# Router and shared expert in plain f32 on unsplit rows, logits by token tiles, modulations of the next block on TensorE, short expert lists first

## The chip, the cores and the metric

One core of a Trainium2 chip. The metric is the device time of one execution in microseconds: 3116.91 us is the median of three runs of the kernel before (3116.86 to 3132.91). TensorE is called PE here (PEld its weight loads), VectorE DVE, ScalarE ACT, GpSimd POOL, SyncE SP.

## The reference

Two blocks run one after the other on 512 tokens of 1024 channels, all in f32. The first has a mixer and a mixture of experts, the second two layers of other mixers and an MLP, each with modulations (shift, scale, gate) that are computed from a conditioning vector. What the change touches is the end of the first block:

```
x = x + gt1 * (heads_x @ w_out)                       # mixer's output projection
h = modulate(rmsnorm(x, g_ffn), sh2, sc2)
scores = sigmoid(h @ router_w)                        # 64 experts
... choose 4 of 8 groups of experts, then 6 experts a token, weights sum to 2.5
routed[t] += w[t, e] * swiglu(h[t], w_gate[e], w_up[e], w_down[e])    # 256 hidden
x = x + gt2 * (routed + swiglu(h, s_gate, s_up, s_down))              # shared expert, 256 hidden
```

and the start of the second: `silu(c_2) @ mod_w_2[layer] + mod_b_2[layer]`, 6 x 1024 columns a layer, in which c_2 is one vector of 1024.

## The kernel before, in words

Activations lie with channels on the partitions (8 tiles of 128 channels x 512 tokens). The kernel is written for a framework that orders the instructions of each engine at build time, by program order as the priority; `issue_after(i)` keeps a block's instructions of an engine behind instruction i.

*Split arithmetic.* Most projections take an f32 value as a sum of two reduced parts: `split` (L307 to 310) writes the high part by ACT (L309) and the rest by POOL or DVE (L310), and `mm3` (L336 to 343) makes three matmuls of it (L338, L342, L343). One step is 128 x 128 weights against 512 columns.

*The end of the mixer* (L665 to 690). The output projection runs in two groups g of four output tiles, each in two column halves i (two of the four token tiles each). After a half of the second group, `second_norm` (L1519) and `norm_half` (L1467) make the norm, write h in split form (`mhh`, `mhl`), transpose it to token rows and store these in DRAM (`hrows`). `shared_ahead` loads the router's and the shared expert's weights and splits them.

*The start of the experts* (`moe`, L1303 to 1400). The logits are 24 split steps with the router's 64 columns as weights, a copy `lt` and four transposes (L1340). `route` (L1072 to 1198) picks the experts, sorts the 64 experts by their number of tokens and gives each token its position in each of its experts' lists. After the first lists are built, the shared expert runs in split form (L1382 to 1399): two column halves of gate and up, then the down projection into x, 144 steps in all.

*Lists.* `slots` (L1210 to 1232) builds the lists of up to eight experts at once: a one-hot per expert on DVE (L1216), four small matmuls on PE (L1218), then small DVE instructions to a tile of sources (L1227, read by the gather), a tile of targets (L1229, read by the scatter) and weights. Empty slots have an out-of-range source, and a spare row behind the 512 as target. These tiles have five buffers each. List lengths are fixed by rank, `CAPS`, four experts each, 128 down to 16 slots (3968 slots in all, for 3072 real rows; the two experts of `TWICE` have a second list). 22 lists are long (over 64 slots), 44 short.

*The loop over 66 lists* (L1420 to 1438), in the order of one long and two short. Per list: POOL gathers the rows by indirect DMA (L1249, three lists ahead), PE transposes them (L1265), ACT copies, PE does gate and up (long L1279; short L1274, in two column groups), ACT does Silu (L1281), DVE the gated product `eh` (L1282), PE transposes it (L1287), DVE copies it to `ehT` (L1288), PE does the down projection (L1295 or L1298), ACT and DVE copy it to `ey` (L1299), and POOL adds it to `yrows` in DRAM by an indirect DMA (L1300). Expert weights are 3 tiles of 1 MB each, on SP's queue, through rings of tiles: 7 are to be had before the shared expert ends (`RINGB`, `ringA`), 15 afterwards (with `RINGD`). The groups of lists are given a due iteration, six lists before their first use (L1352 to 1356), with nothing that holds them there.

*Modulations of the second block.* The first 2048 columns of its first layer are eight pieces of 256 (`MODS_B`): their weights pass through the same rings in the loop, and from iteration 48 on DVE makes the dot products (L396) against a row form of the vector that PE spreads over the partitions (`on_rows`, L404). `mod_rows` (L408) and `mod_cols` (L414) are the form on PE that the first block's own modulations use at the start of the kernel: four matmuls of 32 columns of weights against 512, twice, then four small ones that bring the row back to columns.

The functions that the diff touches, with the lines of the profile:

Of the kernel before, what the change touches and what calls it, by code (L numbers as in the profile page):

```python
# [9 lines left out]
F32 = mybir.dt.float32  # L10
# [10 lines left out]
P = 128  # L21
# [21 lines left out]
HLB = 4  # L43
RINGB = 1
RINGD = 8

CAPS = (128, 128, 96, 80, 72, 64, 56, 48, 48, 40, 40, 32, 32, 24, 24, 16)
MODS_B = 8
# [114 lines left out]
def layout(v):  # L163
# [21 lines left out]
    o["mod_w_2"] = two(lambda l: _rows(g["mod_w_2"][l], (256,) * 24))  # L185
# [26 lines left out]
class Kern:  # L212
# [201 lines left out]
    def mod_cols(self, p, pool, out):  # L414

        r = pool.tile([P, T], F32, tag="mdr", name="mdr", bufs=2)
# [76 lines left out]
    def block1_mix(self):  # L493
# [12 lines left out]

        esr = ExitStack()
# [10 lines left out]

        self.sc32 = ax.tile([P, KD, 32], F32, name="sc32")
        nc.gpsimd.memset(self.sc32, 0.0)  # L520
        nc.vector.tensor_copy(self.sc32[:, :, 0:2], sc2)
        self.pick = ax.tile([P, 2], F32, name="pick")
        nc.vector.tensor_reduce(self.pick, self.ident.rearrange("p (q i) -> p i q", i=32)[:, 0:2], axis=AX.X, op=OP.add)
# [146 lines left out]
        self.hl, self.nhl = [hlB] * HLB + [self.hlS] * 2 + [hlB] * 2, 0  # L670
        self.subs = (nc.gpsimd, nc.vector)
        ks = (4, 5, 6, 7, 0, 1, 2, 3)
        for g in range(2):
            ws = [w for j in range(2) for w in self.split_w(self.load_w(I["w_out"], (2 * g + j) * 256, 256))]
            ps = [self.ps(tag=n) for n in ("c00", "c01", "c10", "c11")]
            for i in range(2):
# [7 lines left out]
                if g:  # L684
                    self.second_norm(i)
                    self.norm_half(i)
        self.shared_ahead()
# [384 lines left out]
    def route(self, logits, R):  # L1072
# [120 lines left out]
        nc.gpsimd.tensor_copy(aux[:, :, :, 0], self.C("pidx").unsqueeze(2).to_broadcast([P, NT, NE]))  # L1193
        for t in range(NT):
            nc.gpsimd.memset(aux[:, t, :, 1], float(t))
        nc.gpsimd.memset(aux[:, :, :, 2], 1.0)
# [13 lines left out]
    def slots(self, pos, aux, n, cap, pool, tag, bufs):  # L1210
# [9 lines left out]
        v, a, iv, u = t_("v", n, 6, k=2), t_("a", n, k=2), t_("iv", n, k=2), t_("u", n, k=2)  # L1220
        src, dst, wt = t_("src", n, dt=I32), t_("dst", n, dt=I32), t_("wt", n)
# [10 lines left out]
        return src, dst, wt  # L1232
# [20 lines left out]
    def expert(self, W, dst, wt, xg, pool):  # L1253
# [28 lines left out]
        nc.vector.scalar_tensor_tensor(h, h, wt, up, op0=OP.mult, op1=OP.mult)  # L1282
# [13 lines left out]
        for n, o in enumerate(os_):  # L1296
            for k in () if pair else range(2):
                mm(o, hT[:, k], wd[:, k, n * T:(n + 1) * T], start=k == 0, stop=k == 1)  # L1298
            (nc.vector.tensor_copy if n else nc.scalar.copy)(y[:, n * T:(n + 1) * T], o)  # L1299
        nc.gpsimd.indirect_dma_start(out=self.yrows, out_offset=bass.IndirectOffsetOnAxis(ap=dst, axis=0), in_=y,  # L1300
                                     in_offset=None, bounds_check=T + P - 1, oob_is_err=True, compute_op=OP.add)

    def moe(self):  # L1303
# [6 lines left out]
        nc.gpsimd.tensor_copy(self.trib, self.C("before"))  # L1310
        nc.gpsimd.tensor_copy(self.onesb, self.C("ones"))
        self.spare = cp.tile([P, 1], F32, name="spare")
        nc.gpsimd.tensor_scalar(self.spare, self.C("pidx"), float(T), None, op0=OP.add)
# [3 lines left out]
        self.alias = {"tp": ["c00", "c01"], "gu": ["c10", "c11"], "y": ["ax", "st0", "st1"], "sl": ["dn"]}  # L1317
        ahead = self.pool("ringA", bufs=6, es=es)
        sp = self.sp = self.pool("slots", es=es)
        es1 = self.es1  # L1320
        self.subs = (nc.gpsimd,)
        self.esh.close()
        h = self.h2
        b = self.pool("moe1", es=es1, side="right")
        self.hlM = self.pool("hlM", bufs=1, es=es1, side="right")
# [3 lines left out]
        for x in self.xgs:  # L1329
            nc.gpsimd.memset(x, 0.0)  # L1330
        for i in range(0, T + P, CAP):
            n = min(CAP, T + P - i)
            nc.scalar.dma_start(self.yrows[i:i + n], self.xgs[0][:n])
        Ws = [self.expert_load(I["experts"][e], ahead, nc.scalar) for e in range(FIRST)]
        self.stream = "y"
        lt = b.tile([NE, T], F32, tag="sg_", name="lt", bufs=2)
        nc.scalar.copy(lt, self.mtile(self.rw, 0, h, m=NE))
        lg = self.ps((P, NT, NE))
        for t in range(NT):
            nc.tensor.transpose(lg[:, t], lt[:, t * P:(t + 1) * P], self.ident[:NE, :NE])  # L1340
        self.stream = "sl"
        self.route(lg, R)
        got = {}

        long, short = [e for e in range(FIRST, NE) if CAPS[e // 4] > 64], [e for e in range(NE) if CAPS[e // 4] <= 64]
# [12 lines left out]
        def sl(e, n, b=0):  # L1358
# [5 lines left out]
            for j, x in enumerate(zip(*[[a[:, j:j + 1] for j in range(n)] for a in self.slots(  # L1364
                    lambda j: pos[:, :, j], lambda j, t: R["aux"][:, t, e + j], n, CAPS[e // 4], sp, "s2" if b else "s", 1 if b else 5)])):
                got[e + j, b] = [q[:CAPS[(e + j) // 4]] for q in x]

        sl(0, 4)
# [10 lines left out]
        ring = [self.pool("ringB", bufs=RINGB, es=esb)] * RINGB + [ahead] * 6  # L1379

        self.hl, self.nhl = [self.hlM, self.hlS, self.hlS, self.hlM], 0
        for j in range(2):  # L1382
            self.wgu[j, 1] = self.split_w(self.raws[j][:, :, P:])[0]
# [37 lines left out]
        for i in range(n + 1):  # L1421
            for g in due.pop(i, ()):
                sl(*g)
# [975 lines left out]
```

## Time and profile before

| | |
|---|---|
| time, three runs | 3116.91 (3116.86 to 3132.91) us |
| the profiled execution's own time | 3115.47 us |
| its span in the profile | 3113.7 us |
| mean granted clock of PE | 0.925 |
| PE busy | 2773.6 us (89%), 17250 instructions |
| PEld busy | 2050.8 us (66%) |
| DVE busy | 1574.9 us (51%), 3396 instructions |
| ACT busy | 951.2 us (31%), 1900 instructions |
| POOL busy | 1094.6 us (35%), 839 instructions |

The span in 40 slices of 77.8 us, busy share in tenths (the DMA line is the mean over the 16 DMA engines); the experts are slices 9 to 17, counted from one:

```profile
PE   6999998799888898678998889989989988889998
...
DVE  5877765642111112375856575663748575642224
...
PEclk9999898899999999969999789999899798999999
DMA  5134002469999999831124114453121041212221
```

A stretch's busy shares are averages; what ends last in it is read from the waits and the timeline. Idle time of an engine that others don't wait for costs nothing.

### The profile page before, as it was taken

What the parts mean: (1) busy time and instruction counts of PE and PEld (TensorE: products, weight loads), DVE (VectorE), ACT (ScalarE), POOL (GpSimd) and SP (SyncE); (2) the same over time, 40 slices, a digit from 0 to 9 for tenths busy, and PEclk for the clock granted to TensorE, in tenths of its full rate; (3) what the DMA queues carried; (4) which work ended last, traced back from release to release, by engine and by line L of the source; (5) the groups of instructions that cost most, each with busy time, mean ns of one, the idle gap of its engine ahead of it and who ended that gap; (6) DMA issues with size and microseconds to landing.
All of it is one profiled execution on the core that took longest, in us unless ns stands there. A gap on an engine that the chain in (4) does not pass through costs nothing.

```text
span 3113.7 us, 44073 instructions
## 1 busy us (share of the span) xinstructions
PE 2773.6 (89%) x17250; PEld 2050.8 (66%) x17250; DVE 1574.9 (51%) x3396; ACT 951.2 (31%) x1900; POOL 1094.6 (35%) x839
## 2 busy tenths in 40 slices
PE   6999998799888898678998889989989988889998
PEld 4767887566544444265665677878856656778887
DVE  5877765642111112375856575663748575642224
ACT  4243333311111111133423343322334234433222
POOL 3333333422222222234333235644252243354443
PEclk9999898899999999969999789999899798999999
DMA  5134002469999999831124114453121041212221
GB/s 215 63 113 156 2 2 99 172 185 379 359 356 340 342 349 374 319 124 42 55 82 149 61 55 173 165 178 113 52 82 41 28 149 54 80 70 95 95 95 55
DMA packets 81537, 460.76 MB, mean 148 GB/s; under 512 B 11424, under 2 KB 18240, under 8 KB 35120
## 3 DMA queue, kind: packets, MB, share of 16 engines
q1 hardware_dynamic: 63360, 404.98, 34.6%
q0 software_dynamic: 11312, 31.46, 4.3%
q10 hardware_dynamic: 6656, 21.50, 1.8%
q8 instruction: 136, 2.23, 0.3%
q14 instruction: 73, 0.60, 0.1%
HBM read 434.29 MB, written 27.26 MB: 148 GB/s over the span
## 4 chain that ended last, share of the span: by engine, by line
PE 35%; DVE 9%; DMA 3%; POOL 2%; issue 2%; ACT 2%; ACTq 0%; DVEq 0%; POOLq 0%
PE ps_pj L338 5%; PE ps_pj L342 5%; PE ps_pj L343 5%; PE ps_a L342 4%; PE ps_a L338 4%; PE ps_a L343 4%; DVE rawm L396 2%; DMA rawm<-in_mod_w_dram 2%; PE ps_a L1695 1%; PE ps_m L1947 1%; PE ps_a L2030 1%; PE ps_a L1685 1%; PE ps_a L1718 1%; DVE bs L2328 1%; DVE ba L2332 1%
## 5 line engine op out<-in xcount | busy, mean ns | idle before, releaser
L310 POOL TENSOR_TENSOR wl<-raw,wh 128x1024 fp32r<-128x1024 f32 (+2 forms) x165 | 408.4, 2477 | 663.5 <-ACT wh L309 628.2
L309 ACT CAST wh<-raw 128x1024 fp32r<-128x1024 f32 (+2 forms) x241 | 246.7, 1034 | 562.4 <-PE ps_a L342 397.2
L338 PE MATMUL ps_pj<-lhh,wh 128*128 128x512 f32 (+5 forms) x816 | 326.4, 400 | 1.8 <-ACT wh L309 1.2
L343 PE MATMUL ps_pj<-lhh,wl 128*128 128x512 f32 (+5 forms) x816 | 315.8, 387 | 6.1 <-POOL wl L310 3.6
L342 PE MATMUL ps_pj<-lhl,wh 128*128 128x512 f32 (+5 forms) x816 | 315.5, 387 | 0.0
L396 DVE SCALAR_TENSOR_TENSOR rawm<-rawm,cb 128x1024 f32<-128x1024 f32 x128 | 206.6, 1631 | 92.7 <-DMA rawm<-in_mod_w_dram 75.3
L310 DVE TENSOR_TENSOR wl<-raw,wh 128x1024 fp32r<-128x1024 f32 x76 | 99.2, 1306 | 206.6 <-ACT wh L309 206.5
L1300 POOL DMA_INDIRECT yrows<-ey,sdst x64 | 97.3, 1520 | 279.9 <-DMA yrows<-ey,sdst 143.8
L338 PE MATMUL ps_a<-lhh,wh 128*128 128x512 f32 (+3 forms) x464 | 169.7, 370 | 21.7 <-ACT lhh L470 13.9
L338 PEld LDWEIGHTS ps_pj<-lhh,wh 128*128 128x128 f32 (+2 forms) x816 | 160.1, 196 | 40.3 <-issue 11.6
L343 PEld LDWEIGHTS ps_pj<-lhh,wl 128*128 128x128 f32 (+2 forms) x816 | 159.3, 195 | 39.4 <-POOL wl L310 4.4
L342 PEld LDWEIGHTS ps_pj<-lhl,wh 128*128 128x128 f32 (+2 forms) x816 | 159.9, 196 | 35.4 <-issue 9.0
L1282 DVE SCALAR_TENSOR_TENSOR eh<-eh,swt,ps_c 128x256 f32<-128x256 f32 (+10 forms) x64 | 30.2, 472 | 288.9 <-ACT eh L1281 287.6
L342 PE MATMUL ps_a<-lhl,wh 128*128 128x512 f32 (+3 forms) x464 | 168.8, 365 | 0.9 <-POOL lhl L474 0.6
L1274 PE MATMUL ps_c<-raw,xT 128*48 128x256 f32 (+6 forms) x1408 | 167.5, 387 | 0.0
L343 PE MATMUL ps_a<-lhh,wl 128*128 128x512 f32 (+3 forms) x464 | 167.5, 362 | 0.0
L1279 PE MATMUL ps_c<-raw,xT 128*128 128x256 f32 (+3 forms) x704 | 161.0, 386 | 0.0
L1279 PEld LDWEIGHTS ps_c<-raw,xT 128*128 128x128 f32 (+3 forms) x704 | 118.9, 172 | 47.2 <-issue 9.9
L1249 POOL DMA_INDIRECT xg<-hrows,ssrc x64 | 66.3, 1036 | 233.5 <-PE ps_c L1265 190.5
L1281 ACT ACTIVATE eh<-ps_c 128x256 f32<-128x256 f32 (+10 forms) x66 | 25.1, 380 | 387.2 <-PE ps_c L1279 217.2
L1274 PEld LDWEIGHTS ps_c<-raw,xT 128*48 128x48 f32 (+6 forms) x1408 | 84.9, 117 | 65.3 <-issue 7.3
L2155 POOL TENSOR_TENSOR ffr<-ffr 128x512 f32<-128x512 f32 x64 | 84.3, 1335 | 114.9 <-ACT ffr L2154 114.9
(875 smaller groups left out, 6377.9 us busy)
## 6 DMA issues: line engine op xcount, KB each, us to landing
raw<-in_experts_dram SPq DMA_DIRECT2D x186, 1024.0 KB
raw<-in_mlp_w_dram SPq DMA_DIRECT2D x64, 1024.0 KB
raw<-in_w_in_dram SPq DMA_DIRECT2D x38, 1024.0 KB
rawm<-in_mod_w_dram SPq DMA_DIRECT2D x28, 1024.0 KB
rawm<-in_mod_w_dram SPq DMA_DIRECT2D x40, 512.0 KB
raw<-in_w_out_dram SPq DMA_DIRECT2D x12, 1024.0 KB
rawm<-in_w_mod_dram SPq DMA_DIRECT2D x20, 512.0 KB
raw<-in_w_mod_dram SPq DMA_DIRECT2D x8, 1024.0 KB
```

The costliest lines, as they stand in the source:

```text
L309: self.nc.scalar.copy(hi, src)
L310: (eng or self.sub_engine()).tensor_sub(lo, src, hi.bitcast(F32))
L338: i = mm(out, wh, xh, start=first, stop=False)
L342: mm(out, wh, xl, start=False, stop=False)
L343: mm(out, wl, xh, start=False, stop=last)
L396: self.nc.vector.scalar_tensor_tensor(raw[:, m], raw[:, m], 1.0, cb, op0=OP.mult, op1=OP.mult, accum_out=out[:, m:m + 1])
L1249: self.nc.gpsimd.indirect_dma_start(out=xg, out_offset=None, in_=self.hrows, in_offset=bass.IndirectOffsetOnAxis(ap=src, axis=0), bounds_c ...
L1274: mm(o, xT[:, k], w[:, k], start=k == 0, stop=k == KD - 1)
L1279: mm(o, xT[:, k], w[:, k], start=k == 0, stop=k == KD - 1)
L1300: nc.gpsimd.indirect_dma_start(out=self.yrows, out_offset=bass.IndirectOffsetOnAxis(ap=dst, axis=0), in_=y, in_offset=None, bounds_check=T ...
L1685: nc.tensor.transpose(p[:, j], e[:, j * P:(j + 1) * P], self.ident)
L2155: nc.gpsimd.tensor_mul(r, r, r)
```

## The change

- **Unsplit rows.** `norm_half` writes h once, in f32. The split copies of h, the router's weights and the shared expert's weights go, with their pools; the ring for the shared expert's weights has 3 tiles instead of 2, and `shared_ahead` (loads only) moves ahead of the first `second_norm`.
- **Logits by token tiles.** Right behind each h tile, plain f32 matmuls with a token tile as weights against the router's 64 columns: 32 in all, two halves of 16. The copy `lt` and the four transposes go.
- **Shared expert in plain f32.** 48 matmuls of 512 columns; the first half of gate and up stands right behind `route`, the rest behind the first lists.
- **Modulations on PE.** The first 2048 columns of the second block's first layer are loaded as eight tiles of 1 MB on SP's queue ahead of the experts, and made with `mod_rows` and `mod_cols` ahead of `route`. The eight pieces, their dots and `on_rows` leave the loop.
- **Queues and engines.** The first two experts' tiles go from ACT's queue to SP's, behind the modulations. Casts and zeroing go from POOL to ACT, the `aux` fills from POOL to DVE. `yrows` has 512 rows (four zeroing transfers, not five).
- **Rings.** RINGB 5 and RINGD 5: 11 tiles before the shared expert ends, 16 afterwards.
- **Lists.** No targets: the scatter uses the sources, and out-of-range rows are dropped. The order is two short, then one long, with the doubled experts after eight long ones. Up front, groups (0, 2), (20, 4) and (4, 4): 10 lists (14 before). In the loop, each of the nine groups is held behind the latest gated product.

```
-HLB = 4
-RINGB = 1
-RINGD = 8
+HLB = 6
+RINGB = 5
+RINGD = 5
...
+    def columns(self, pool, sc):
+        nc = self.nc
+        self.sc32 = pool.tile([P, KD, 32], F32, name="sc32")
+        nc.vector.memset(self.sc32, 0.0)
+        nc.vector.tensor_copy(self.sc32[:, :, 0:sc.shape[2]], sc)
...
     def slots(...)
-        src, dst, wt = t_("src", n, dt=I32), t_("dst", n, dt=I32), t_("wt", n)
+        src, wt = t_("src", n, dt=I32), t_("wt", n)
...
-        nc.vector.scalar_tensor_tensor(u, iv, BIG, a, op0=OP.mult, op1=OP.add)
-        nc.vector.tensor_copy(src, u)
-        nc.vector.scalar_tensor_tensor(u, iv, self.spare[:cap], a, op0=OP.mult, op1=OP.add)
-        nc.vector.tensor_copy(dst, u)
+        nc.vector.scalar_tensor_tensor(a, iv, BIG, a, op0=OP.mult, op1=OP.add)
+        nc.vector.tensor_copy(src, a)
...
     def expert(...)
-        nc.vector.scalar_tensor_tensor(h, h, wt, up, op0=OP.mult, op1=OP.mult)
+        self.gated = nc.vector.scalar_tensor_tensor(h, h, wt, up, op0=OP.mult, op1=OP.mult)
...
-        nc.gpsimd.indirect_dma_start(out=self.yrows, out_offset=bass.IndirectOffsetOnAxis(ap=dst, axis=0), in_=y,
-                                     in_offset=None, bounds_check=T + P - 1, oob_is_err=True, compute_op=OP.add)
+        nc.gpsimd.indirect_dma_start(out=self.yrows, out_offset=bass.IndirectOffsetOnAxis(ap=src, axis=0), in_=y,
+                                     in_offset=None, bounds_check=T - 1, oob_is_err=False, compute_op=OP.add)
...
     def moe(self):
+        n = MODS_0 // 256
+        raws = [(ring[0] if i < RINGB else ahead).tile([P, KD * RING_W], F32, tag="raw", name="rawm") for i in range(n)]
+        for i, raw in enumerate(raws):
+            self.loaded = nc.sync.dma_start(raw, I["mod_w_2"][0][:, 2048 * i:2048 * i + 2048])
...
+        for i, raw in enumerate(raws):
+            if i % 2 == 0:
+                p = self.ps()
+            self.mod_rows(p, raw.rearrange("p (q n) -> p q n", q=4), i % 2)
+            if i % 2:
+                self.mod_cols(p, b, pm[:, 2 * (i - 1):2 * (i + 1)])
+        nc.vector.tensor_add(self.mod2[0][:, :2 * n], pm[:, :, 0], self.V("mod_b_2", 0, 2 * n))
+        Ws = dict(enumerate(self.expert_load(I["experts"][e], ahead) for e in range(FIRST)))
         self.stream = "sl"
+        self.route(self.lg, R)
...
+        def gate_up(m):
+            p = [self.ps(tag="gu"), self.ps(tag="gu")]
+            for k in range(KD):
+                for q, w in zip(p, self.ws):
+                    nc.tensor.matmul(q, w[:, k, m * P:(m + 1) * P], h[:, k], start=k == 0, stop=k == KD - 1)
+            nc.scalar.activation(s_h[:, m], p[0], AF.Silu)
+            nc.vector.tensor_mul(s_h[:, m], s_h[:, m], p[1])
+
+        gate_up(0)
...
+        long = [e for e in range(FIRST, NE) if CAPS[e // 4] > 64 and e not in TWICE]
+        m = len(long)
+        long[8:8] = TWICE
+        short = [e for e in range(NE) if CAPS[e // 4] <= 64]
         seq = list(range(FIRST))
         while long or short:
-            seq += long[:1] + short[:2]
+            seq += short[:2] + long[:1]
             del long[:1], short[:2]
...
-        groups = [(e, 4 if e in (0, 60) else 8, 0) for e in (0,) + tuple(range(4, NE, 8))] + [(TWICE[0], len(TWICE), 1)]
+        groups = [(0, FIRST, 0), (4 + m, 4, 0), (4, 4, 0)] + [(TWICE[0], len(TWICE), q) for q in range(2)]
+        groups += [(e, min(8, 4 + m - e), 0) for e in range(8, 4 + m, 8)] + [(e, min(8, NE - e), 0) for e in range(8 + m, NE, 8)]
...
         for i in range(n + 1):
             for g in due.pop(i, ()):
-                sl(*g)
+                with self.tc.issue_after(self.gated.ins) if i else ExitStack():
+                    sl(*g)
...
-            if i == 48:
-                self.cb = self.on_rows(b2, lambda k: self.sc_2[:, k:k + 1])
-            if i >= 50 and i % 4 == 0:
-                self.pend.pop(0)()
...
     def norm_half(self, i):
+            self.lg = self.ps((P, NT, NE), tag="lg")
...
+            hk = halves(self.h2[:, k], i)
...
-            self.split(halves(h[0][:, k], i), halves(h[1][:, k], i), hk, nc.gpsimd)
+            for t in range(2):
+                nc.tensor.matmul(self.lg[:, HALF_OF[i][t]], hk[:, t], self.rw[:, k], start=(i, k, t) == (0, 0, 0), stop=(i, k, t) == (1, KD - 1, 1))
...
     def shared_ahead(self):
+        self.rw = self.mr.tile([P, KD, NE], F32, name="rw")
+        self.nc.sync.dma_start(self.rw.rearrange("p k e -> p (k e)"), I["router_w"])
+        self.ws = [self.load_w(I["shared"], c, 256) for c in (0, 256, 512)]
```

## Rows read from the trace of the kernel before

**Rows 1.** Stretches of 520 to 1313 us: us, each engine's busy (count), PEclk, DMA share, GB/s.

```profile
520.00:557.00 37.00, 36.38 (x303) 35.40 (x303) 15.02 (x39) 11.78 (x29) 13.29 (x17) 1.00 0.19 58
...
557.00:640.00 83.00, 64.08 (x335) 47.67 (x334) 55.37 (x162) 20.91 (x39) 32.00 (x34) 0.84 0.48 176
...
640.00:1313.00 673.00, 588.32 (x3504) 320.30 (x3504) 131.17 (x341) 102.18 (x264) 163.39 (x127) 0.96 0.95 343
...
1230.00:1290.00 60.00, 51.59 (x394) 21.99 (x392) 14.92 (x32) 9.93 (x30) 16.33 (x12) 1.00 1.02 401
```

**Rows 2.** Waits, 624 to 1326: engine, line waited for, us in total, times, longest.

```profile
POOL yrows L1300 <- DMA yrows<-ey,sdst: 143.8, 24, 8.7
...
PE ps_c L1287 <- DVE eh L1282: 40.7, 17, 8.7
...
DVE sdst L1229 <- DMA yrows<-ey,sdst: 35.8, 3, 15.1
...
DVE ssrc L1227 <- DMA xg<-hrows,ssrc: 18.0, 2, 9.7
...
PEld ps_c L1279 <- DMA raw<-in_experts_dram: 5.8, 7, 0.8
```

**Rows 3.** Timeline of one stall: start us, us, engine, line, [idle before <-releaser].

```profile
835.66 0.16 DVE L1229 CAST sdst<-su 32x8 int32<-32x8 f32 x1 [15.12 <-DMA yrows<-ey,sdst]
...
837.14 0.41 PE L1287 MATMUL ps_c<-const_all,eh 48*128 48x48 f32 x2 [8.67 <-DVE eh L1282]
```

**Rows 4.** Timeline of PE: first and last expert matmuls, starts of neighbouring lists.

```profile
640.46 0.60 PE L1279 MATMUL ps_c<-raw,xT 128*128 128x256 f32 x2
...
1190.98 7.13 PE L1279 MATMUL ps_c<-raw,xT 128*72 128x256 f32 x32
...
1204.89 3.64 PE L1274 MATMUL ps_c<-raw,xT 128*24 128x256 f32 x32
...
1278.65 3.63 PE L1274 MATMUL ps_c<-raw,xT 128*16 128x256 f32 x32
...
1286.14 3.63 PE L1274 MATMUL ps_c<-raw,xT 128*16 128x256 f32 x32
...
1310.45 2.52 PE L1295 MATMUL ps_st<-raw,ehT 128*16 128x512 f32 x8 [0.95 <-DVE ehT L1288]
```

**Rows 5.** Timeline of PE: unit costs of matmul shapes; xN counts records.

```profile
22.83 3.64 PE L412 MATMUL ps_ps<-raw,sc 128*32 128x512 f32 x16
...
40.44 1.06 PE L412 MATMUL ps_ps<-raw,sc 128*32 128x512 f32 x8
...
44.85 1.50 PE L419 MATMUL ps_ps<-pick,mdr 128*128 128x2 f32 x8
...
611.02 1.24 PE L1173 MATMUL ps_c<-rx,rT 64*128 64x64 f32 x8
...
618.07 0.40 PE L338 MATMUL ps_c<-mhh,wh 128*128 128x512 f32 x1
...
618.30 0.40 PE L342 MATMUL ps_c<-mhl,wh 128*128 128x512 f32 x1
...
655.89 1.88 PE L1298 MATMUL ps_st<-raw,ehT 128*128 128x512 f32 x4
...
657.61 1.88 PE L1298 MATMUL ps_ax<-raw,ehT 128*128 128x512 f32 x4
```

**Rows 6.** Groups by line, 624 to 1326: busy us, mean ns, idle before.

```profile
L404 PE MATMUL ps_c<-const_all,sc 128*128 128x128 f32 x16 | 2.5, 291 | 0.7 <-DVE eh L1282 0.7
```

**Rows 7.** Line 1216: count, shortest/median/longest ns, first to last start, shapes.

```profile
L1216 DVE TENSOR_TENSOR oneh<-const_moe,Rpos x64: 202/349/693, 612.7 to 802.6; 128x512 bf16<-128x512 f32 x12, 128x256 bf16<-128x256 f32 x8, 128x192 bf16<-128x192 f32 x8, 128x160 bf16<-128x160 f32 x8
```

**Rows 8.** DMA queues of the page: packets, MB, share of 16 engines' span.

```profile
q0 software_dynamic: 11312, 31.46, 4.3%
```

**Rows 9.** Timeline of POOL: the first and the last scatter of the lists.

```profile
661.11 1.63 POOL L1300 DMA_INDIRECT yrows<-ey,sdst  x1 [11.00 <-ACT xT L1266]
...
1315.31 1.30 POOL L1300 DMA_INDIRECT yrows<-ey,sdst  x1 [2.60 <-DVE ey L1299]
```

More of the change, by code (lines that the diff above doesn't have):

```diff
@@ L517, in block1_mix @@
         ct = ax.tile([P, KD, TC], F32, name="ct")
[L519 to L523, printed above, removed]
+        self.columns(ax, sc2)
         nc.sync.dma_start(ct, I["ctxT"])
@@ L1251, in gather, with expert @@
         return xg
-    def expert(self, W, dst, wt, xg, pool):
+    def expert(self, W, src, wt, xg, pool):
         nc = self.nc
@@ L1309, in moe @@
         self.onesb = cp.tile([P, P], BF, name="onesb")
[L1310 to L1313, printed above, removed]
+        nc.scalar.copy(self.trib, self.C("before"))
+        nc.scalar.copy(self.onesb, self.C("ones"))
         R = {n: cp.tile([P] + s, F32, name="R" + n) for n, s in
@@ L1316, in moe @@
         R["eidi"] = cp.tile([1, NE], I32, name="Reidi")
[L1317 removed]
+        self.alias = {"tp": ["c00", "c01"], "gu": ["c10", "c11"], "y": ["st1", "st0", "ax"], "sl": ["dn"]}
         ahead = self.pool("ringA", bufs=6, es=es)
+        ring = [self.pool("ringB", bufs=RINGB, es=es)] * RINGB + [ahead] * 6
         sp = self.sp = self.pool("slots", es=es)
         es1 = self.es1
[L1321 to L1322 removed]
         h = self.h2
         b = self.pool("moe1", es=es1, side="right")
[L1325 removed]
+        self.columns(cp, bcl(self.sc_2, 1))
         R["aux"] = cp.tile([P, NT, NE, 6], BF, name="Raux")
@@ L1329, in moe @@
         for x in self.xgs:
[L1330 to L1334, printed above, removed]
-        self.stream = "y"
[L1336 to L1340, printed above, removed]
@@ L1341, in moe @@
-        self.stream = "sl"
-        self.route(lg, R)
+            nc.scalar.activation(x, self.x[:, :2].rearrange("p k t -> p (k t)"), AF.Copy, scale=0.0)
+        for i in range(0, T, CAP):
+            nc.scalar.dma_start(self.yrows[i:i + CAP], self.xgs[0])
+        n = MODS_0 // 256
+        raws = [(ring[0] if i < RINGB else ahead).tile([P, KD * RING_W], F32, tag="raw", name="rawm") for i in range(n)]
+        for i, raw in enumerate(raws):
+            self.loaded = nc.sync.dma_start(raw, I["mod_w_2"][0][:, 2048 * i:2048 * i + 2048])
@@ L1378, in moe @@
         esb = ExitStack()
[L1379 to L1383, printed above, removed]
-        wd = self.split_w(self.load_w(I["shared"], 512, 256).rearrange("p a b -> p (a b)").rearrange("p (k n) -> p k n", k=2))
-        Ws = dict(enumerate(Ws))
-        Ws[FIRST] = self.expert_any(R["eidi"][:, FIRST:FIRST + 1], ring, self.loaded)
-        s_h = [b.tile([P, 2, T], F32R, name=n) for n in ("s_hh", "s_hl")]
-        self.stream = "gu"
-        for m in range(2):
-            g = b.tile([P, T], F32, tag="sg_", name="sg_", bufs=2)
-            nc.scalar.activation(g, self.mtile(self.wgu[0, m], 0, h), AF.Silu)
-            nc.vector.tensor_mul(g, g, self.mtile(self.wgu[1, m], 0, h))
-            self.split(s_h[0][:, m], s_h[1][:, m], g)
+        wd = self.ws[2].rearrange("p a b -> p (a b)").rearrange("p (k n) -> p k n", k=2)
+        e = seq[FIRST]
+        Ws[e] = self.expert_any(R["eidi"][:, e:e + 1], ring, self.loaded)
+        gate_up(1)
         for m in range(KD):
@@ L1396, in moe @@
             for k in range(2):
-                c = slice(m % 4 * P, m % 4 * P + P)
-                self.mm3(p, wd[m // 4][0][:, k, c], wd[m // 4][1][:, k, c], s_h[0][:, k], s_h[1][:, k], k == 0, k == 1)
+                nc.tensor.matmul(p, wd[:, k, m * P:(m + 1) * P], s_h[:, k], start=k == 0, stop=k == 1)
             nc.vector.scalar_tensor_tensor(self.x[:, m], p, self.gt2[:, m:m + 1], self.x[:, m], op0=OP.mult, op1=OP.add)
@@ L1438, in moe @@
                     pass
-        for f in self.pend:
-            f()
         nc.vector.tensor_copy(left, R["nov"])
@@ L1444, in moe @@
         with self.tc.For_i(0, n, 1):
-            src, dst, wt, eid = self.overflow(R, ov, b2)
-            for _ in self.expert(self.expert_any(eid, ahead), dst, wt, self.gather(src), b2):
+            src, wt, eid = self.overflow(R, ov, b2)
+            for _ in self.expert(self.expert_any(eid, ahead), src, wt, self.gather(src), b2):
                 pass
```

71 lines of the change are left out of this document (30 added, 41 removed).

## The prediction

> **What bounds the kernel now.** I read the slices of the page first (they find the stretch that the change touches), then the stage table, then the waits of that stretch, then the timeline of single stalls. The stage table [rows 1] cuts the stretch in three. From 520 to 557 us, the tail of the mixer's output projection, TensorE (PE) is busy 36.38 of 37.00 us at full clock: whatever is added there is paid in full. From 557 to 640, router, lists and shared expert, it is busy 64.08 of 83.00 at a granted clock of 0.84: 18.9 us are idle. From 640 to 1313, the expert lists, it is busy 588.32 of 673.00 with the DMA engines at 0.95 of theirs, so two suspects stand side by side.
>
> The waits separate them [rows 2]. PE lost 5.8 us in seven waits on expert weights, so weights land in time and the transfers are not what ends last; near the end of the stretch the same queues move 401 GB/s against 343 on average [rows 1]. What PE does wait for is `eh`, the gated product on VectorE (DVE): 40.7 us in 17 waits, the longest 8.7. DVE in turn stood still for 35.8 us in three waits at the cast of a new list of targets (L1229), until the scatter that read the old one had ended, and for 18.0 us in two at the cast of sources (L1227). The timeline shows one [rows 3]: the cast of 835.66 waited 15.12 us, the copy and the gated product behind it ran late, and PE's transpose of `eh` waited 8.67.
>
> What the lists cost without such stalls is read from pairs of starts late in the stretch [rows 4]: a long list (over 64 slots) 1204.89 - 1190.98 = 13.91 us, a short one 1286.14 - 1278.65 = 7.49. There are 22 long and 44 short: 22 x 13.91 + 44 x 7.49 = 635.6. The stretch took 1310.45 + 2.52 - 640.46 = 672.5 [rows 4], so 36.9 us are lost, in five stalls, the lower clock after them and the modulation dots among the last lists. The pair for the long list has 72 slots; lists of 128 have longer transposes, so 36.9 is an upper bound.
>
> **The change part by part.** The sum goes against the profiled execution, 3115.47 us, 1.4 below the median of 3116.91.
>
> *Logits by token tiles.* 32 plain f32 matmuls of 64 columns. Four such (eight records), those that start at 611.02, took 1.24 [rows 5], so 0.31 each. The 16 of the first half fall before 557, where PE is full: +5.0. The 16 of the second half (5.0) replace 24 steps on split rows at 0.23 (618.30 - 618.07, [rows 5]), 5.5: -0.5.
>
> *Shared expert in plain f32.* 48 matmuls of 512 columns. The starts 655.89 and 657.61 bound two of them, four records [rows 5]: 1.72, 0.86 each, 41.3 in all. They replace 144 steps at 0.23, 33.1: +8.2. The split copies that vanish ran on ACT, DVE and POOL; I count nothing for them but the idle time below.
>
> The Trainium skill ("FP8 and Floating Point Precision", section "TensorE Precision Notes") says that true FP32 takes four passes through the array. An estimate by that would be 4/3 of 33.1, 44.1, and the forecast 3 us later; the rows of this trace say 41.3, and I go by them.
>
> *Modulations on PE.* Eight pieces of four matmuls and four groups of four small ones. A piece took between 1.06 and half of 3.64 [rows 5], a small group 1.50 (1.87 at the slow clock I take as the upper end): 8 x 1.06 + 4 x 1.50 = 14.5 to 8 x 1.82 + 4 x 1.87 = 22.0. I take 16, near the lower end, since the clock before 557 is full. The eight 1 MB loads move 8.4 MB ahead of the experts' first six tiles on SP's queue: 8.4 + 6.3 MB at 401 GB/s is 37 us of transfers, in a stretch whose DMA share is 0.19 to 0.48; the first expert's weights are wanted at 640 or later. I count nothing; without that cover it is up to 21 us (8.4 MB / 401).
>
> *The start of the lists.* 8.2 + 16 - 0.5 = 23.7 of added PE work behind 557, of which the idle 18.9 takes its part: +4.8, with the 5.0 of the logits **+9.8**. If no idle time is used it is +28.7. If the full clock comes back with the split waits gone, 64.08 x (1 - 0.84) = 10.3 is regained: -0.5. I take 9.8, between them, because PE's order in this stretch is fixed and now has independent work (modulations) to put into the router's idle time. The small moves (aux copies POOL to DVE, casts and zeroing POOL to ACT, one zero transfer less) fall on engines busy 55.37 and 20.91 of the 83.00 us [rows 1]; nothing.
>
> *Lists at their turn.* Short groups come first, each later group is held behind a gated product and has buffers free by then, and the second list (targets) with its cast is gone. The waits of L1227 and L1229 go, and the dots and their loads leave the loop: up to **-36.9**; below, nothing gained if the stalls only change place (rivals). What is new is DVE work in the steady state: nine groups, each some eight one-hots of 0.349 (0.693 the longest, [rows 7]) and some eight small instructions like the cast of 0.16 [rows 3], so 4.1 to 6.8 us. Queued behind it on DVE are `ehT` of the list under way and the `ey` copies; PE's cover meanwhile is the next short list's gate and up, 3.64 [rows 4]. Past the cover stand 0.4 to 3.2; I take 0.9, since most lists are short: **+8.1**.
>
> *Row form of the conditioning.* 16 matmuls of L404 leave the loop: 2.5 us [rows 6]: **-2.5**.
>
> *Eleven tiles ahead, 16 instead of 15 later.* Against 5.8 us of waits this is worth at most that; I count nothing. DMA need afterwards: 673 us x 343 GB/s = 230.8 MB, less 8.4 of modulations and 3.7 of padding rows (3968 slots, 3072 real rows, 4 KB each), 218.7 MB in some 636 us, 344 GB/s: the rate of now.
>
> *Sum:* 3115.47 + 9.8 - 36.9 + 8.1 - 2.5 = 3094.0; with the 1.4 to the median, **3095**.
>
> **Rivals.**
>
> *R1, the chain of scatters binds.* Each scatter-add is issued when the one before has landed: POOL waited 143.8 us for that in 24 waits [rows 2], and 66 run from 661.11 to 1315.31 [rows 9], one per 10.06. Dropped padding saves 3.7 of 31.46 MB of that queue, whose packets took 4.3% of the span, 133.9 us [rows 8]: 15.6, or 0.24 a scatter. If the chain sets the pace, the stretch falls only by that: 3115.5 - 15.6 + 9.8 + 1.4 = 3111. For it: the long total. Against it: with 7.49 for a short list over long stretches the chain followed. The Trainium skill ("DMA: Bandwidth & Descriptors", section "Queues, rings and completion order") has each DMA engine alternate between queues packet by packet, by which deeper loading would lengthen scatters; no row of before shows it. Chance 0.13.
>
> *R2, nothing of the front is hidden.* PE's order puts modulations and shared expert where PE was busy: +28.7 in place of 9.8, 3114. For it: the logits wait for the last square, so what is idle then stays idle. Chance 0.14.
>
> *R3, all is hidden.* Front -0.5, no new stalls: 3115.5 - 0.5 - 36.9 - 2.5 + 1.4 = 3077. For it: the groups are small, the clock would stay up. Chance 0.17.
>
> *R4, the groups stall the lists (slower).* Held behind the gated product, a group sits on DVE ahead of `ehT`, and PE cannot go to the down projection. Priced like the five stalls of now, 36.9 / 5 = 7.4 each: nine cost 66.6 in place of 8.1: 3154. It decides from 3.3 us a group ((21.5 + 8.1) / 9), where the time of before is reached. Against it: 0.4 to 3.2 above. Chance 0.11.
>
> **How the numbers follow.** Forecast 0.45, its own range 3080 to 3108. I take 0.5% (15.6 us) as what can be told from no change: faster is under 3101, slower over 3132. Faster: 0.38 of the forecast, R3's 0.17 and 0.07 of R1 and R2, 0.62. Slower: most of R4, 0.10. Same: the rest, 0.28. The range takes in R3 with its clock bound, R1 and R2 with some of the lost load cover: 3067 to 3125.
>
> **What would show it.** The first expert matmul near 650 (R2: 668, R3: 640). Waits of PE for `eh` under 10 us and no wait of a DVE cast for a DMA; if DVE's one-hots appear as releaser of `ehT` in the loop, R4. The pitch of the lists stays at 13.9 and 7.5; if POOL's wait for the last scatter grows and PE waits behind `ey`, R1. Modulation matmuls between 557 and 640. Wrong altogether, if PE waits on weights over 20 us in the loop.

## The result, and the profile after

The changed kernel takes 3082.52 us (median of four runs, 3069.76 to 3086.04) against 3122.87 for the kernel before on the same chip: a ratio of 0.986, 95% interval 0.982 to 0.990. A second series gave 3077.53 against 3113.64, 0.988 (0.986 to 0.990). The forecast was 3095 in a range of 3067 to 3125: the side and the range hold, but the way there was nearer to that of the rival R3 than to that of the forecast. The gain was forecast at 21.9 us (3116.91 - 3095) and measured at 40.4 and, in the second series, 36.1. The execution that was profiled took 3069.76 us.

The stage table of the changed kernel (columns as in [rows 1]); the last row ends at 1260, so that only lists lie in it:

```profile
557.00:640.00 83.00, 76.81 (x380) 41.75 (x379) 39.45 (x154) 16.89 (x31) 6.49 (x7) 0.92 0.77 292
640.00:1260.00 620.00, 570.18 (x3475) 315.38 (x3473) 118.47 (x313) 100.15 (x260) 153.46 (x126) 0.99 0.95 347
```

The same last stretch of the kernel before:

```profile
640.00:1260.00 620.00, 547.11 (x3210) 304.22 (x3210) 111.72 (x299) 94.60 (x242) 149.07 (x120) 0.96 0.96 343
```

Between 557 and 640 PE is now busy 76.81 us instead of 64.08, at 0.92 instead of 0.84 of its clock: more work went into the same 83 us. Among the lists it is busy 23 us more of the same 620, at 0.99 instead of 0.96, while the transfers run at the rate they had, 347 against 343 GB/s.

The waits of the changed kernel from 624 to 1290 us, those that answer to [rows 2] (engine, line waited for, us in total, times, longest):

```profile
POOL yrows L1309 <- DMA yrows<-ey,ssrc: 171.7, 28, 9.8
ACT ey L1308 <- DMA yrows<-ey,ssrc: 44.5, 11, 7.9
PE ps_c L1274 <- ACT xT L1275: 16.2, 19, 2.2
PE ps_c L1296 <- ACT xT L1275: 14.5, 18, 1.6
PE ps_c L1296 <- DVE eh L1291: 9.6, 10, 1.1
```

PE's wait for `eh` fell from 40.7 us to 9.6, its longest from 8.7 to 1.1, and no cast of a list waits for a DMA any more. POOL waits longer for the scatter before, 171.7 us against 143.8, and the lists are faster all the same: that chain followed.

PE's timeline, first gate and last down matmul, and marks between them that the text below uses (start us, us, engine, line, [idle before <-releaser]):

```profile
562.35 0.66 PE L1526 MATMUL ps_dn<-const_all,sq 128*128 128x1 f32 x4
...
628.70 1.88 PE L1415 MATMUL ps_c<-s_h,raw 128*128 128x512 f32 x4
630.41 1.88 PE L1415 MATMUL ps_st<-s_h,raw 128*128 128x512 f32 x4
...
642.97 7.07 PE L1288 MATMUL ps_c<-raw,xT 128*128 128x256 f32 x32
...
689.16 0.65 PE L1283 MATMUL ps_c<-raw,xT 128*64 128x256 f32 x2
689.74 0.44 PE L1296 MATMUL ps_c<-const_all,eh 128*128 128x128 f32 x2
690.11 3.67 PE L1283 MATMUL ps_c<-raw,xT 128*64 128x256 f32 x30
...
715.06 0.65 PE L1283 MATMUL ps_c<-raw,xT 128*56 128x256 f32 x4
...
1198.31 7.13 PE L1288 MATMUL ps_c<-raw,xT 128*72 128x256 f32 x32
...
1212.11 3.64 PE L1283 MATMUL ps_c<-raw,xT 128*24 128x256 f32 x32
...
1261.34 0.29 PE L1296 MATMUL ps_c<-const_all,eh 16*128 16x16 f32 x2 [1.01 <-DVE eh L1291]
...
1268.82 1.90 PE L1304 MATMUL ps_st<-raw,ehT 128*16 128x512 f32 x8 [0.28 <-DVE ehT L1297]
```

The lists take 1268.82 + 1.90 - 642.97 = 627.8 us, against 672.5 [rows 4]. That is 44.8 us less, where the two profiled executions differ by 45.7 in all. The lists begin 2.5 us later (642.97 against 640.46), and what runs behind them is shorter by the rest.

### The profile page after: what moved, and what is told of

The parts are those of the page before. It is cut to its first block, busy times and chain, and to the rows that moved or that the text cites. A ratio compares the mean times of both kernels' runs of the same rounds, so it can differ in the third digit from the quotient of the medians.

```text
span 3067.6 us, 44111 instructions
## 1 busy us (share of the span) xinstructions
PE 2778.7 (91%) x17318; PEld 2044.9 (67%) x17318; DVE 1522.5 (50%) x3358; ACT 944.0 (31%) x1882; POOL 1044.5 (34%) x803
## 4 chain that ended last, share of the span: by engine, by line
PE 35%; DVE 9%; DMA 3%; POOL 2%; ACT 2%; issue 2%; ACTq 0%; DVEq 0%; POOLq 0%
PE ps_pj L341 5%; PE ps_pj L345 5%; PE ps_pj L346 5%; PE ps_a L345 4%; PE ps_a L341 4%; PE ps_a L346 4%; DMA rawm<-in_mod_w_dram 3%; DVE rawm L399 2%; PE ps_a L1694 1%; DVE ba L2331 1%; PE ps_m L1946 1%; PE ps_a L2029 1%; PE ps_a L1684 1%; PE ps_a L1717 1%; PE ps_a L1815 1%
## 5 line engine op out<-in xcount | busy, mean ns | idle before, releaser
L313 POOL TENSOR_TENSOR wl<-raw,wh 128x1024 fp32r<-128x1024 f32 (+1 forms) x161 | 395.8, 2461 | 718.3 <-ACT wh L312 670.9
L312 ACT CAST wh<-raw 128x1024 fp32r<-128x1024 f32 (+1 forms) x235 | 240.5, 1034 | 500.3 <-PE ps_a L345 354.1
L313 DVE TENSOR_TENSOR wl<-raw,wh 128x1024 fp32r<-128x1024 f32 x74 | 126.0, 1702 | 208.4 <-ACT wh L312 208.4
L399 DVE SCALAR_TENSOR_TENSOR rawm<-rawm,cb 128x1024 f32<-128x1024 f32 x112 | 166.9, 1507 | 105.8 <-DMA rawm<-in_mod_w_dram 87.3
L1309 POOL DMA_INDIRECT yrows<-ey,ssrc x60 | 86.0, 1433 | 308.7 <-DMA yrows<-ey,ssrc 166.3
L1291 DVE SCALAR_TENSOR_TENSOR eh<-eh,swt,ps_c 48x256 f32<-48x256 f32 (+10 forms) x60 | 28.4, 473 | 279.4 <-ACT eh L1290 277.1
L341 PEld LDWEIGHTS ps_a<-lhh,wh 128*128 128x128 f32 x464 | 94.7, 206 | 31.0 <-ACT lhh L482 15.6
L345 PE MATMUL ps_a<-ffl,wh 128*128 128x512 f32 (+1 forms) x288 | 106.6, 370 | 7.9 <-DVE ffl L313 7.9
```

What stands on the lines that cost most here:

```text
L312: self.nc.scalar.copy(hi, src)
L313: (eng or self.sub_engine()).tensor_sub(lo, src, hi.bitcast(F32))
L341: i = mm(out, wh, xh, start=first, stop=False)
L345: mm(out, wh, xl, start=False, stop=False)
L399: self.nc.vector.scalar_tensor_tensor(raw[:, m], raw[:, m], 1.0, cb, op0=OP.mult, op1=OP.mult, accum_out=out[:, m:m + 1])
```

## The experiments

In the table, "lists" is the time from the first gate matmul to the end of the last down matmul of the profiled execution, worked out as just now; "start" is that first matmul. Two profiles of the unaltered changed kernel gave 627.8 and 631.7 us, and e6, in which no instruction of the lists was altered, 636.2: differences of this total below some 8 us say little by themselves, and what a part does is read where it does it. The kernel before has one profile. Ratios go to the kernel before, on the chip of that series.

| run | start | lists | median us | ratio (95%) |
|---|---|---|---|---|
| before | 640.46 | 672.5 | | |
| changed | 642.97 | 627.8 | 3082.5 | 0.986 (0.982 to 0.990) |
| e1, before + hold | 643.25 | 649.4 | 3098.7 | 0.990 (0.986 to 0.994) |
| e2, before, no targets | 637.66 | 658.1 | 3111.4 | 0.996 (0.995 to 0.998) |
| e3, before, no modulations in the loop | 645.25 | 664.7 | 3110.9 | 0.996 (0.994 to 0.998) |
| e4, changed, no hold | 639.28 | 630.2 | 3071.0 | 0.981 (0.978 to 0.985) |
| e5, changed again | 639.76 | 631.7 | 3077.5 | 0.988 (0.986 to 0.990) |
| e6, changed, no modulations | 635.67 | 636.2 | 3065.0 | 0.985 (0.983 to 0.987) |
| e7, changed, long first | 644.53 | 631.6 | 3075.3 | 0.988 (0.985 to 0.990) |
| e8, changed, 7 tiles | 640.97 | 638.3 | 3076.5 | 0.990 (0.987 to 0.993) |
| e9, changed, no hold, long first | 641.65 | 633.7 | 3079.7 | 0.987 (0.984 to 0.990) |
| e10, before + three parts | 646.79 | 645.2 | 3087.1 | 0.988 (0.986 to 0.991) |
| e11, changed, three ey | 640.12 | 620.8 | 3075.5 | 0.986 (0.983 to 0.988) |
| e12, three ey, gate first | 644.39 | 623.9 | 3071.7 | 0.984 (0.982 to 0.986) |

**e1: the hold alone, on the kernel before.**

```
+        self.gated = nc.vector.scalar_tensor_tensor(h, h, wt, up, ...)
...
-                sl(*g)
+                with self.tc.issue_after(self.gated.ins) if i else ExitStack():
+                    sl(*g)
```

> The kernel before with one part of the change alone: each group of lists in the loop is held behind the latest gated product. Theory (the stalls come from lists that are built too early, so that their casts wait for DMAs that still read the old list): the waits of L1227 and L1229 on DMAs, 53.8 us, go to under 10, the stretch of the lists falls by 20 to 37 us, and the time by as much (ratio 0.988 to 0.993). Rival (a group behind the gated product stalls the lists itself): ratio 1.00 or above, DVE's one-hots stand ahead of ehT. Rival (the dots and the loads of the modulations cause the loss): under 8 us, ratio 0.997 to 1.

The lists fell by 23.2 us. The waits of casts on DMAs are gone, and of PE's wait for `eh` this is left:

```profile
PE ps_c L1287 <- DVE eh L1282: 13.7, 11, 1.9
```

The theory holds, and R4 falls: groups behind the gated product don't stall the lists at its price, 7.4 us each.

**e2: no targets, alone.** In `slots`, `dst = src`, with the target cast and its sum gone; the scatter has `bounds_check=T - 1, oob_is_err=False`.

> The kernel before with one part of the change alone: no list of targets, the scatter uses the sources and drops out-of-range rows. Theory: the list tile is now read by gather and scatter both, so the cast that writes it waits as long; the stalls stay, and only the padding rows are saved: 0 to 8 us, ratio 0.997 to 1. Rival (the second tile and its cast are the cause): 20 us or more, ratio 0.993 or less.

```profile
DVE ssrc L1228 <- DMA yrows<-ey,ssrc: 35.2, 3, 15.1
PE ps_c L1286 <- DVE eh L1281: 32.5, 17, 8.6
```

As expected the wait moved from the target cast to the source cast, 35.2 us in three against 35.8 in three. The other two waits, 18.0 us on gathers, are gone, and the lists are 14.4 us shorter, more than the 8 that I gave to the padding rows: right on where the wait goes, too low on the size, with the difference unexplained.

**e3: no modulations in the loop.** Their loads, dots and row form are left out, and a constant stands in the 2048 columns.

```
-        self.pend = self.mods(0, range(0, MODS_B * 256, 256), [ring] * MODS_B)
+        self.pend = []
+        nc.vector.memset(self.mod2[0], 0.01)
...
```

> The kernel before without the first 2048 modulation columns of the second block's first layer: their loads, row form and dots are left out, a constant stands in. Theory: the stalls at 828 to 1008 us stay, since the dots come later; 3 to 10 us are won at the tail and by the 8.4 MB, ratio 0.996 to 0.999. Rival (dots and loads in the loop are what costs): 20 us or more, ratio 0.993 or less.

7.9 us of lists, within what the theory gave, though no more than this measure differs by from profile to profile; the casts wait as before:

```profile
DVE sdst L1229 <- DMA yrows<-ey,sdst: 35.0, 3, 14.1
DVE ssrc L1227 <- DMA xg<-hrows,ssrc: 17.7, 2, 9.7
```

**e4 and e9: the hold taken out of the changed kernel, and with it the new order.** e4 has `sl(*g)` without the hold; e9 has besides `seq += long[:1] + short[:2]`.

> The changed kernel with the hold behind the gated product taken out; the framework's order decides when lists are built. Theory: the lists are built early again, casts wait for DMAs, and 15 to 37 us of the gain go: ratio to before 0.991 to 0.999. Rival (order of the lists, smaller first groups and the missing targets are enough): the time of the changed kernel, ratio 0.985 to 0.988, and no wait of a cast for a DMA.

> The changed kernel without the hold and with the old order of the lists. Each alone left the lists at 630 to 632 us. Theory (either of the two is enough to keep the casts out of the way of the transfers, so only both together bring the stalls back): 645 us or more for the lists, 13 us or more lost, and casts that wait for scatters by 30 us or more. Rival (neither matters, the smaller first groups and the buffers of their own for the first experts do it): 628 to 635 us.

Both theories miss. The rival of e4 misses too, since casts do wait; that of e9, 628 to 635 us, has its number. Without the hold the lists are built early again, and two casts wait for scatters in either kernel; of e4:

```profile
DVE ssrc L1238 <- DMA yrows<-ey,ssrc: 18.4, 2, 9.7
PE ps_c L1296 <- DVE eh L1291: 14.0, 12, 3.4
```

The lists take 630.2 and 633.7 us in all, which can't be told from 627.8 and 631.7. But that total hides two parts that cancel, as the time between the `eh` transposes of one list and those of a later one shows. From the 13th list to the 22nd e4 is slower, 103.2 us against 90.3; first the changed kernel, then e4 (columns as in [rows 1]):

```profile
763.38:853.63 90.25, 81.35 (x484) 44.56 (x483) 16.41 (x43) 14.25 (x36) 23.08 (x20) 0.98 1.02 365
763.26:866.44 103.18, 91.47 (x555) 49.44 (x555) 21.46 (x80) 14.13 (x36) 22.00 (x18) 0.91 1.01 367
```

From the 28th to the 31st it is faster, 32.1 us against 36.5, since the changed kernel builds a group there and e4 has built it long before:

```profile
912.67:949.21 36.54, 36.36 (x184) 23.28 (x184) 7.37 (x24) 5.02 (x13) 6.50 (x5) 0.91 1.01 376
924.95:957.03 32.08, 31.90 (x152) 20.38 (x152) 4.60 (x9) 5.02 (x13) 6.47 (x5) 1.00 0.98 361
```

The changed kernel's PE makes the small matmuls for that group's one-hots there, and the next long list's gate takes 9.20 us at a lower granted clock, where 7.07 is usual:

```profile
913.83 0.50 PE L1229 MATMUL ps_dn<-Raux,oneh 128*40 128x6 bf16 x12
916.98 9.20 PE L1288 MATMUL ps_c<-raw,xT 128*128 128x256 f32 x32
```

The same comes again from the 52nd list to the 55th, 28.4 us in e4 against 32.3. e9 and e7, both with the old order, show the same: 104.2 against 92.4 from the 13th to the 22nd, and 28.4 against 30.8 from the 52nd to the 55th. So in the changed kernel the hold moves the cost of building lists to a later place and wins nothing in sum; e4's ratio is even the lowest of the table, which e9, with 0.987, doesn't bear out. Why early building costs less here than in the kernel before isn't the order (e9). The smaller first groups, the buffers that experts 0 to 3 have for themselves and the missing targets are left; they weren't tried apart.

**e5, e7: the changed kernel again, and with the old order of lists.**

> The changed kernel unaltered, as the one to which the others of this series are compared. Both theories: the expert lists take 626 to 630 us from the first gate matmul to the last down matmul, as in its first profile (627.8), and what varies from run to run lies behind them (ratio 0.982 to 0.990).

> The changed kernel with the old order of the lists, one long and then two short. Theory (with the lists built at their turn the order is worth little): the stretch of the lists 0 to 5 us longer. Rival (short ones first is what gives the second half of the gain): 10 us or more, and waits of POOL or DVE on scatters in the first 100 us.

631.7 and 631.6: the order of the lists is worth nothing that shows here. The two profiled executions of the unaltered kernel differ by 11.8 us of span, of which 4.0 are in the lists. By the starts of the same instructions, the two keep within 5 us of each other for 1150 us behind the first block's end, and then 11 us come up in one stretch of the second block, at another granted clock. First the changed kernel's first profile, then e5's:

```profile
2430.00:2760.00 330.00, 295.43 (x1596) 231.37 (x1597) 184.26 (x418) 126.29 (x264) 130.21 (x81) 0.92 0.24 83
```

```profile
2430.00:2760.00 330.00, 292.39 (x1549) 228.64 (x1548) 185.53 (x420) 123.27 (x260) 126.65 (x80) 0.88 0.22 80
```

So single totals of this kernel spread by more than most parts of the change are worth, and the lists' own time is the better measure, if not a sharp one.

**e6: no modulations ahead of the router.** Loads, matmuls and sums are left out; the bias alone stands in the 2048 columns.

```
...
-            self.mod_rows(p, raw.rearrange("p (q n) -> p q n", q=4), i % 2)
-            if i % 2:
-                self.mod_cols(p, b, pm[:, 2 * (i - 1):2 * (i + 1)])
-        nc.vector.tensor_add(self.mod2[0][:, :2 * n], pm[:, :, 0], self.V("mod_b_2", 0, 2 * n))
+        nc.vector.tensor_copy(self.mod2[0][:, :2 * n], self.V("mod_b_2", 0, 2 * n))
```

> The changed kernel without the 2048 modulation columns that it makes ahead of the router (loads, matmuls, sums); the bias alone stands in. Theory (they fill PE time that was idle, and lift its clock): the first gate matmul comes 0 to 6 us earlier, the time falls by as much. Rival (they stand on PE's path one for one): 14 to 22 us earlier.

The last norm matmul and the first gate matmul of e6:

```profile
563.81 0.58 PE L1516 MATMUL ps_dn<-const_all,sq 128*128 128x1 f32 x4
...
635.67 0.81 PE L1288 MATMUL ps_c<-raw,xT 128*128 128x256 f32 x3
```

71.9 us between them, against 642.97 - 562.35 = 80.6 with the modulations (79.6 in e5): they cost 8 to 9 us, between the two expectations. In the changed kernel their matmuls keep PE busy for 9.15 us (L415) and 3.74 (L431), 12.9 in all, so the 16 that I gave them was too much, and some 4 us are covered. From the end of the last norm matmul to the first gate matmul, first in e6, then in the changed kernel:

```profile
564.39:635.67 71.28, 63.11 (x257) 33.51 (x257) 38.28 (x145) 12.23 (x23) 5.21 (x5) 0.90 0.59 213
563.01:642.97 79.96, 74.28 (x353) 38.56 (x353) 38.39 (x146) 14.52 (x27) 5.30 (x5) 0.92 0.74 282
```

PE's idle time falls from 8.2 to 5.7 us, so 2.5 us of the cover are idle time that they fill; where the rest of it lies isn't shown. The lists of e6 are 4.5 to 8.4 us longer than in the two profiles with modulations, at a granted clock of 0.97 against 0.99 and 0.98.

**e8: 7 tiles before the shared expert ends.** `RINGB = 1`, `RINGD = 9`.

> The changed kernel with 7 weight tiles before the shared expert ends instead of 11 (RINGB 1, RINGD 9; 16 afterwards as before). Theory (weights landed 10 us and more before use): 0 to 4 us longer. Rival (the modulations push the experts' tiles back, so the extra four tiles are needed): PE waits on experts' weights by 10 us or more in the first lists.

The lists took 638.3 us, 6.5 and 10.5 more than the two profiles with 11 tiles. The loss stands in the first six lists. From the `eh` transposes of the first list to those of the seventh, first in the changed kernel (54.5 in e5 too), then in e8:

```profile
651.58:706.06 54.48, 54.48 (x334) 34.17 (x332) 12.49 (x33) 10.14 (x24) 13.45 (x12) 1.00 0.89 323
649.57:713.99 64.42, 55.01 (x332) 34.00 (x330) 12.49 (x33) 10.24 (x24) 15.74 (x13) 0.97 0.87 309
```

That is 9.9 us, and PE, which had no idle time there, has 9.4. Waits for weights in the first 120 us:

```profile
PE ps_c L1283 <- DMA raw<-in_experts_dram: 4.7, 2, 3.4
PE ps_c L1288 <- DMA raw<-in_experts_dram: 0.6, 1, 0.6
```

and, in the 60 us with most of them, the granted clock; first e8, then the changed kernel:

```profile
700.00:760.00 60.00, 51.13 (x281) 31.79 (x282) 11.78 (x30) 8.74 (x22) 9.94 (x8) 0.89 1.02 378
```

```profile
700.00:760.00 60.00, 57.13 (x366) 34.66 (x364) 13.49 (x33) 9.98 (x24) 16.12 (x13) 1.00 1.02 366
```

Neither theory fits: the waits, 5.3 us, are half of the rival's 10 us, but shorter waits for `xT` come with them, the clock fell after them, and the loss is more than they are. The medians, 3076.47 and 3077.53, don't show it; e8's runs lie between 3067.07 and 3099.14, further apart than the loss.

**e10: hold, no targets and no modulations together, on the kernel before** (the edits of e1 to e3).

> The kernel before with three parts of the change together: groups held behind the gated product, no targets, and no modulations in the loop (left out, a constant stands in). Alone they took 23.2, 14.4 and 7.9 us off the 672.5 us of the lists. Theory (hold and missing targets remove the same stalls, the dots stand apart): 636 to 644 us for the lists, the rest of the gain is tiles ahead and order. Rival (they add up): 624 to 630 us, nothing left to explain.

645.2 us, 27.3 less than before, where the three alone sum to 45.5. That is 1.2 us above the theory's 636 to 644 and far from the rival's 624 to 630: in the main they remove the same stalls. The medians agree: 22.6, 9.9 and 10.5 us alone, 32.5 together. From e10 to e7, which has the same order of lists, 13.6 us are missing, and nearly all of them in the first six lists. From the `eh` transposes of the first to those of the seventh, first e10, then e7:

```profile
655.47:727.56 72.09, 65.11 (x335) 43.04 (x335) 15.07 (x33) 11.29 (x25) 14.47 (x12) 0.98 0.71 239
652.77:711.87 59.10, 59.10 (x334) 38.66 (x333) 12.63 (x33) 10.54 (x25) 13.67 (x11) 1.00 0.86 309
```

There PE waits for weights in e10 as it does in e8, 5.3 us in three waits, and never in e7.

**e11 and e12: two steps further.** e11 has `name="ey", bufs=3`. e12 besides puts `next(runs[i])` (gate and up) ahead of `next(runs[i - 1])` (the transposes of `eh`) in the loop.

> The changed kernel with three buffers of ey instead of two, so that ACT's copy waits less for the scatter of two lists before (44.5 us in 11 waits in its profile), and with it the copies of xT that PE waits for (27 us in 33 waits). Theory (those copies are late because ACT stood at ey): the lists 3 to 10 us shorter, PE's waits on xT halved. Rival (the copies wait for PE's own transposes, whatever ey does; the chain of scatters stays): no change within 2 us.

> The changed kernel with three buffers of ey, and with the next list's gate and up placed ahead of the transposes of eh of the list under way (two steps of the loop exchanged), so that Silu and the gated product run under them. Theory (each of some 30 short lists in the second half of the stretch shows a gap of 0.8 to 1.1 us ahead of the transposes, for the way through ACT and DVE): 598 to 612 us for the lists, against 620.8 with the third buffer alone. Rival (the weights' transfers, 347 GB/s now, are next: PE then waits for experts' weights by as much): 616 us or more.

e11's waits, to be laid beside those of the changed kernel:

```profile
ACT ey L1308 <- DMA yrows<-ey,ssrc: 3.4, 1, 3.4
PE ps_c L1274 <- ACT xT L1275: 15.2, 19, 1.1
PE ps_c L1296 <- ACT xT L1275: 7.2, 13, 1.1
```

ACT's waits for scatters went from 44.5 to 3.4 us, and the lists from 627.8 and 631.7 to 620.8. The lists are 7 to 11 us shorter, where the theory gave 3 to 10; of PE's waits on xT only one of two halved. e12's 623.9, with the third buffer too, is also below every profile with two. In e12 the gaps that it was to close stand where they were:

```profile
1258.89 0.29 PE L1296 MATMUL ps_c<-const_all,eh 16*128 16x16 f32 x2 [1.01 <-DVE eh L1291]
```

623.9 us: a miss. The exchange in the program didn't change the order of these instructions at the end of the stretch, and PE's waits for weights were 2.6 us, so neither theory was put to the test. The ratios to the kernel before are 0.986 and 0.984, where the changed kernel had 0.986 and 0.988 in its two series. That e11 and e12 beat it in the total is likely by the lists and not shown.

## Why the prediction was right, and where it was not

**What bounds the stretch: right, but for the first lists.** Late list casts lost most of the time. e1 shows it by one edit: the 53.8 us of DVE waits gone, 23.2 us of lists won. In the first six lists it is the weights, once the casts are out of the way (e8). The DMA need, put at 344 GB/s, came out at 347.

**Unit costs: right for the shared expert, too high for the rest.** Its f32 step was put at 0.86 us; two of them take 630.41 - 628.70 = 1.71 at the full clock. The estimate from the four passes of the Trainium skill ("FP8 and Floating Point Precision", section "TensorE Precision Notes"), 44.1 us for all 48, doesn't show in these rows, which make it 41. The modulations, put at 16 us, take 12.9. Their small groups of 1.50 were read where the granted clock was 0.63 (44.85 to 46.35); in the changed kernel such a group takes 0.95 (595.13). The 1.87 that I called the slow clock stands in rows with a granted clock of 1.00 (27.17 to 29.04); why it took that long isn't shown. The first half of the logits, put at 5.0, shows as 1.9: from the first of the norm's matmuls to the end of the last, with these logits between them, are 20.9 us instead of 19.0.

**The start of the lists, +9.8: wrong.** The eight profiles with the new front (all but e6) start the lists at 641.7 on average (639.3 to 644.5), the five with the old one at 642.7 (637.7 to 646.8): the term is -1, not +9.8. It failed in the step "of which the idle 18.9 takes its part". The idle time did take it: in the 83 us from 557, PE is busy 12.7 us more. But I set 23.7 us of added work against it, at the old clock and with unit costs that were too high, and the clock rose from 0.84 to 0.92; its return, 10.3 us by my own sum, I had given only to R3. The last norm matmul of the kernel before:

```profile
559.20 0.58 PE L1527 MATMUL ps_dn<-const_all,sq 128*128 128x1 f32 x4
```

From it to the first gate matmul are 640.46 - 559.20 = 81.3 us, in e6, without the modulations, 71.9: logits and shared expert on unsplit rows made the front some 9 us shorter, where I had 8.2 - 0.5 = 7.7 of added work; the modulations then took 8 to 9 back. PE's idle time there, from the end of that matmul, is 17.9 us before and 8.2 in e6:

```profile
559.78:640.46 80.68, 62.82 (x325) 46.69 (x325) 55.33 (x161) 19.19 (x35) 29.70 (x30) 0.83 0.48 178
```

That it was the split copies that PE waited for is argued from this and not shown by an edit of its own; I had counted nothing for them but the idle time.

**The lists, -31.3: too small; measured -44.8 and -40.8.** One term, put at nothing, was the main miss.

*The stalls, the groups and the row form, -36.9 + 8.1 - 2.5:* e10, which has these parts, took 27.3 off, near the 31.3. That the terms are each right isn't shown by it.

*The groups at their turn, +8.1:* PE's longest wait for `eh` is 1.1 us, the way through ACT and DVE of the last lists, so the cost doesn't show where I had priced it, in DVE's queue ahead of `ehT`. Yet about this much shows against e4, in the small matmuls that PE makes for a group and in the lower clock behind them: 4.4 us from the 28th list to the 31st and 3.9 from the 52nd to the 55th. The size came out right by luck.

*Eleven tiles ahead, 0:* some 10 (e8, in the first six lists). I had only the 5.8 us of waits in the kernel before; once its first lists are no longer held up, they catch up with the weights, as e1, e8 and e10 show by PE's waits for weights (4.4 to 5.3 us, and none in the kernel before).

*The stall-free sum, 635.6 us:* it isn't the floor that I took it for, nor 36.9 the upper bound of what was lost. The pitches from the end of the stretch hold there (1212.11 - 1198.31 = 13.80 for the long list), but early lists are closer: two short and a long one take 715.06 - 689.16 = 25.9 us, where the late pitches give 28.9. The transposes of `eh` stand two records into the next list's gate (689.74), so the way through ACT and DVE is covered; at the end PE waits about 1 us a list for it (1261.34). The trace of the kernel before had such a place too: its seventh list to its tenth, a long one and two short, takes 747.00 - 720.11 = 26.9 us between the transposes of `eh`.

**The account.** Of 42.8 us (the mean of the two profiles), 27.3 are hold, targets and modulations, taken together on the kernel before (e10); taken out of the changed kernel, the hold alone is worth nothing in sum (e4). Of the 13.6 from e10 to e7, 13.0 stand in the first six lists, where the tiles alone are worth 9.9 (e8). The 5 or 6 us that are left of the 42.8 are no more than profiles of one kernel differ by; smaller groups, their buffers and the moved queues and small instructions are what is left of the change, and weren't tried.

**The rivals.** R3 (front hidden, no new stalls, 3077) is nearest to what happened; I gave it 0.17. It had the start of the lists and the clock right, and nothing for the tiles or the groups. R1: POOL's waits grew to 171.7 us, but e11 shortened the lists without touching the scatters. The Trainium skill ("DMA: Bandwidth & Descriptors", section "Queues, rings and completion order") has each DMA engine take turns between queues packet by packet; whether more loads in flight lengthen scatters by that, no run here isolates. R2 and R4 fall with the start of the lists and with e1.

## What to carry to other kernels

When a queue's order is fixed at build time, look for small writes that land in the bookkeeping of transfers still under way: the wait shows at the cast, the loss on the engine behind it. Removing parts one by one can overstate each: three parts worth 45.5 us alone were worth 27.3 together. A total that doesn't move can hide two parts that cancel, as with the hold in the changed kernel, so compare stretch by stretch. And a pitch read at one end of a loop is no floor for the other end; read it at both.

## What was not expected of the hardware

The granted clock in the second block's stretch of 2430 to 2760 us was 0.92 in one execution of the changed kernel and 0.88 in another, and 11 us of difference in the total came from there, with the same program. A few short waits for weights (5.3 us in e8) went with a clock of 0.89 instead of 1.00 over 60 us. And one group of small matmuls among the lists, with 0.2 us of idle time from the 28th list to the 31st, went with 0.91 there, in both profiles of the changed kernel, where e4 without it had 1.00.
